# Modulation rows of the next layer formed beside the down projection, sums of weights formed before the up stage, and an eighth bank of products

## The chip, the cores and the metric

One core of a Trainium2 chip runs the whole program. The metric is the device time of one execution in microseconds; the median of several executions is compared. Engines are called PE (TensorE), DVE (VectorE), ACT (ScalarE), POOL (GpSimd) and SP (SyncE, which here only gives out DMAs).

## What is computed

A model of two layers over 1024 latent tokens and 256 context tokens, width 1024. What the change touches is the second half of a layer and the modulation (cut from the reference):

```python
for l in range(DEPTH):                      # DEPTH = 2
    need_ctx = l < DEPTH - 1                # context tokens only in layer 0
    sh1, sc1, g1, sh2, sc2, g2 = jnp.split(cond_lat @ w_mod[l] + b_mod[l], 6, axis=-1)
    csh1, csc1, cg1, csh2, csc2, cg2 = jnp.split(cond_ctx @ w_mod[l] + b_mod[l], 6, axis=-1)
    ...
    h = h + g1 * (mix_lat @ w_out[l])
    h = h + g2 * conv_ffn(modulate(rms_norm(h, norm2_g[l]), sh2, sc2), w_up[l], ..., w_down[l])
def conv_ffn(t, w_up, conv_w, conv_b, w_down):
    u = dwconv(t @ w_up, conv_w, conv_b, FFN_PAD[0], FFN_PAD[1])
    g, v = jnp.split(u, 2, axis=-1)         # D_FF = 2816 columns each
    return (jax.nn.silu(g) * v) @ w_down
```

Inputs and output are float32; w_mod has 1024 x 6144 elements a layer.

## The kernel before, in words

Tokens lie along the free dimension in three chunks: A and B of 512 latent tokens each and c of 256 context tokens (layer 0 alone). A tile is 128 rows of output columns. Every float32 factor is split into a rounded part and a rest (hi and lo, `split`, L318 to 323: ACT writes hi, POOL or DVE subtracts for lo), and a product is three matmuls: hi x hi, hi x lo, lo x hi.

A layer runs in five stages: input projection, attention, out projection (`out_proj`), up (`UpProj`), down (`down_proj`).

**Up.** 22 tiles j, each of a gate half (g, z = 0) and a value half (v, z = 1). The products over the chunks A and B go by seven sub-products (`part`, L196) of 4 x 3 matmuls of 512 columns each, in place of eight: over halves of the contraction, sums and differences of weights (`sums_g`, `sums_v`, names s1 to s4) meet sums and differences of inputs (names t1 to t4, formed by `norm` for chunk B from those of A and B). Parts 1 and 2 need only chunk A's inputs; parts 6, 3, 7, 4, 5 those of chunk B in the order t2, 22, t3, t4, t1. In layer 0 two products over the context (`context`, 24 matmuls of 256 columns) come on top. DVE adds the parts up into `fr`; then the convolution over tokens (`conv`: ACT, two DVE ops on 1282 columns, for g and for v; silu; one multiply) gives y, which is stored to DRAM (`ysp`, L241). Weights come over SP into places of 4096 bytes a partition that are used in turn (`unit`: ten in layer 0, fourteen in layer 1), two for a load with its hi part; `plain` loads and splits, `sums_g` and `sums_v` load, form sums on DVE and POOL and split. `early` loads the first of them in the out stage, `ahead` issues first products while chunk B's norm is still going on. Banks of PSUM are taken in turn from `RING`.

**Down.** Tiles of y and of w_down are fetched two tiles ahead (`fetch`), split, and multiplied in groups of two tiles: for each chunk eight outputs n (slots), 6 matmuls each; DVE adds each bank to h in SBUF (`add`, L316), in the first group ACT copies it to `da` and DVE or POOL adds. The last group, with the norm of the next layer behind it, is the returned function `last`.

**Modulation rows.** `mod_rows(l, js, width, bufs)` is a generator that forms cond @ w_mod of layer 1 without the matmul over k: it loads 128 rows k of w_mod (`mraw`), and DVE multiplies by the column of cond and adds up (`macc`, L567 the first, L316 the others); after eight k a matmul with ones sums over partitions (L580), a copy (L583, `ms`), small transposes (L313) and an add of the bias (L592) bring the row to columns. With js = range(6) and width 512 this is sixteen blocks of eight steps: for j < 2 with 256 columns and two accumulators (latent and context), then with 512 columns and one. A `yield` stands before every step and at the pauses. `run` advances it two steps at four places of a tile; the rest is drawn behind the stage.

Instructions are given to a scheduler that keeps the order of the program roughly and moves them by its own priorities; all engines and SP then run their lists in order. What it did is shown below where it matters.

Of the kernel before, what the change touches and what calls it, by code (L numbers as in the profile page):

```python
# [9 lines left out]
F32 = mybir.dt.float32  # L10
# [44 lines left out]
class UpProj:  # L55
# [6 lines left out]
    RING = (0, 1, 2, 3, 4, 5, 6)  # L62
# [25 lines left out]
    def norm(self, ch):  # L88
# [30 lines left out]
        nc.vector.tensor_tensor(d, b.mod[l][:, 3, 0, 4:8], b.mod[l][:, 3, 0, 0:4], op=OP.subtract)  # L119
        for k in range(4):  # L120
            t1, t2, t3, t4, x2 = (f[q][k] for q in ("t1", "t2", "t3", "t4", "22"))
            scaled(t3, k)
            nc.vector.tensor_tensor(t1, t3, t1, op=OP.subtract)
            scaled(x2, k + 4)
            b.stt(t2, x2, sh(k + 4), t1, OP.add, OP.subtract)
            b.stt(t3, x2, d[:, k:k + 1], t3, OP.add, OP.subtract)
            b.stt(t4, t4, sh(k + 4), t2, OP.add, OP.subtract)
            both("22", k, x2, sh(k + 4))
            for t in ("t2", "t3", "t4", "t1"):
                hi, lo = self.x[t][k]  # L130
                b.split(hi, lo, f[t][k], pool_lo=t in ("t1", "t4"))
# [86 lines left out]
    def ahead(self):  # L218
        for j, n in ((0, 1), (1, 1), (0, 2), (1, 2)):
            self.late.append(self.context(0, n - 1) if self.cs and j else self.part(j, n))  # L220
            yield

    def early(self):
        self.plain(0, 0)
        self.plain(0, 1)
        if not self.cs:
            self.plain(1, 0)

    def conv(self, j, z):
# [11 lines left out]
        b.nc.sync.dma_start(b.ysp[j][:, a0 - PC:a1 - PC], g[:, a0:a1])  # L241

    def run(self, fillers):
# [4 lines left out]

        def fill(n):
            for _ in range(n):  # L250
                next(fillers, None)
        n = 4 if self.cs else 3
        for take in self.late[:n]:
            take()
        for j in range(NH):
            if j == 1:
                for take in self.late[n:]:
                    take()
# [4 lines left out]
            if j:  # L263
                self.plain(j, 1)
            if (self.cs or j) and j < NH - 1:
                self.plain(j + 1, 0)
            if j == 0:
                self.sums_g(0)
                self.sums_v(0)
            if j < NH - 1:  # L270
                self.sums_g(j + 1)
            fill(2)
            self.part(j, 6)()
            self.part(j, 3)()
            if 0 < j < NH - 1:
                self.sums_v(j + 1)
            fill(2)
            self.part(j, 7)()
            self.part(j, 4)()
            if j == 0:  # L280
                self.sums_v(1)
            else:
                self.context(j, 1)()
            fill(2)
            self.part(j, 5)()
            fill(2)
            self.conv(j, 0)
            self.conv(j, 1)


class Builder:
# [249 lines left out]
    def mod_rows(self, l, js, width, bufs):  # L541
# [15 lines left out]
        for i in range(len(bufs)):  # L557
            load(i)
        for i, (j, cs, w, c0, k) in enumerate(todo):
# [10 lines left out]
            load(i + len(bufs))  # L570
            if k < KT - 1:
                continue
            yield
            yield
# [9 lines left out]
            yield  # L584
# [659 lines left out]
    def down_proj(self, l, chunks):  # L1244
# [35 lines left out]
        def group(js, parts, ring, evac):  # L1280
            for ch in parts:
                c0, m = CHUNKS[ch]
                g = self.mod[l][:, 5, 1 if ch == "c" else 0]
                for n in range(KT):
                    ps = self.bank(ring[ch] if isinstance(ring, dict) else ring)[:, :m]
                    self.gemm(ps, [term(j, n, ch) for j in js])
                    evac(n, ch, ps, g[:, n:n + 1], self.h[n][:, c0:c0 + m])
                yield ch
# [61 lines left out]
    def build(self, ctx):  # L1350
# [38 lines left out]
        for l in range(DEPTH):  # L1389
            need = l < DEPTH - 1  # L1390
            chunks = ("A", "B", "c") if need else ("A", "B")
            if l:
                first = self.first_weights(l)
# [56 lines left out]
```

## Time and profile before

| | before |
|---|---|
| runs, us | 3114.69, 3118.12, 3119.87 (median 3118.12) |
| profiled execution, us | 3120.11 |
| its span from the first to the last instruction, us | 3118.3 |
| mean granted clock of TensorE | 0.964 |
| PE, DVE, ACT, POOL busy, us | 2859.0, 2289.3, 1398.5, 1228.1 |
| HBM read and written, MB | 243.02, 54.02 |

A stage is read from the stretches in which its tiles appear: in layer 0 the out projection lies at about 640 to 777 us of the span, the up stage to 1452, the down stage to 1786; in layer 1 the up stage at 2409 to 2846 and the down stage behind it. "Busy" is time in which an engine works on at least one instruction; successive instructions of an engine overlap by some tens of nanoseconds. The granted clock is the share of TensorE's full speed that the profile shows for the stretch: 1.0 is 2.4 GHz, 0.5 is 1.2 GHz.

### The profile page before, as it was taken

What the parts mean: (1) busy time and instruction counts of PE and PEld (TensorE: products, weight loads), DVE (VectorE), ACT (ScalarE), POOL (GpSimd) and SP (SyncE); (2) the same over time, 40 slices, a digit from 0 to 9 for tenths busy, and PEclk for the clock granted to TensorE, in tenths of its full rate; (3) what the DMA queues carried; (4) which work ended last, traced back from release to release, by engine and by line L of the source; (5) the groups of instructions that cost most, each with busy time, mean ns of one, the idle gap of its engine ahead of it and who ended that gap; (6) DMA issues with size and microseconds to landing.
All of it is one profiled execution on the core that took longest, in us unless ns stands there. A gap on an engine that the chain in (4) does not pass through costs nothing.

```text
span 3118.3 us, 38974 instructions
## 1 busy us (share of the span) xinstructions
PE 2859.0 (92%) x14523; PEld 2283.4 (73%) x14523; DVE 2289.3 (73%) x3098; ACT 1398.5 (45%) x2198; POOL 1228.1 (39%) x726
## 2 busy tenths in 40 slices
PE   7999988899789889889999998998899899999998
PEld 4668855578578678767788866876567688887787
DVE  5676798877878787878666767789745876666766
ACT  4675477733323232234211366557753443444213
POOL 1211266542544434444411121137653666665210
PEclk8999999999899899999999999999999899999999
DMA  7413200142234345456312210110022344445221
GB/s 257 137 61 100 64 14 5 44 137 79 87 110 125 104 137 150 129 152 216 135 63 77 75 34 28 50 60 14 21 75 78 88 128 128 122 123 191 95 95 55
DMA packets 295775, 299.57 MB, mean 96 GB/s; under 512 B 16586, under 2 KB 250658, under 8 KB 295586
## 3 DMA queue, kind: packets, MB, share of 16 engines
q1 hardware_dynamic: 295586, 297.09, 29.9%
q8 instruction: 114, 1.87, 0.2%
q14 instruction: 75, 0.61, 0.1%
HBM read 243.02 MB, written 54.02 MB: 95 GB/s over the span
## 4 chain that ended last, share of the span: by engine, by line
PE 52%; DVE 25%; DMA 8%; ACT 7%; issue 5%; POOL 2%; SPq 0%; DVEq 0%; ACTq 0%; POOLq 0%
PE bank L310 51%; DVE cv L316 4%; DMA wr<-in_w_up 3%; DMA mraw<-in_w_mod 3%; ACT lru L307 2%; DVE macc L316 2%; DVE lru L316 2%; DVE mt L994 2%; PE bank L313 1%; ACT cv L307 1%; ACT L307 1%; DVE fr L208 1%; DVE mt L998 1%; DVE xt L323 1%; DVE y L1087 1%
## 5 line engine op out<-in xcount | busy, mean ns | idle before, releaser
L321 POOL TENSOR_TENSOR w<-wr,w 128x1024 fp32r<-128x1024 f32 (+1 forms) x220 | 560.6, 2567 | 518.6 <-ACT w L307 467.4
L310 PE MATMUL bank<-y,w 128*128 128x512 f32 (+1 forms) x2688 | 566.9, 372 | 10.0 <-DVE h L316 9.3
L310 PE MATMUL bank<-xt,w 128*128 128x512 f32 x2112 | 530.7, 405 | 37.2 <-POOL w L321 10.6
L310 PEld LDWEIGHTS bank<-y,w 128*128 128x128 f32 x2688 | 468.7, 190 | 105.2 <-DVE h L316 11.2
L310 PEld LDWEIGHTS bank<-xt,w 128*128 128x128 f32 x2112 | 408.2, 196 | 136.0 <-POOL w L321 14.5
L307 ACT ACTIVATE w<-wr 128x1024 fp32r<-128x1024 f32 (+1 forms) x220 | 223.4, 1018 | 548.3 <-POOL wr L168 377.7
L1054 POOL TENSOR_TENSOR ph<-pf,ph 128x512 fp32r<-128x512 f32 x256 | 341.0, 1354 | 309.2 <-PE bank L310 159.9
L316 DVE SCALAR_TENSOR_TENSOR h<-bank,mod,h 128x512 f32<-128x512 f32 (+1 forms) x448 | 302.9, 687 | 200.3 <-PE bank L310 199.6
L310 PE MATMUL bank<-a,w 128*128 128x512 f32 x1536 | 388.8, 405 | 9.9 <-ACT a L307 2.4
L310 PE MATMUL bank<-x,w 128*128 128x512 f32 x1584 | 394.3, 400 | 2.5 <-DVE fr L208 1.7
L316 DVE SCALAR_TENSOR_TENSOR cv<-fr,fcol,cv 128x1282 f32<-128x1282 f32 (+1 forms) x176 | 320.1, 1877 | 55.0 <-ACT cv L307 55.0
L310 PEld LDWEIGHTS bank<-x,w 128*128 128x128 f32 x1584 | 303.7, 194 | 68.6 <-DVE fr L208 2.6
L310 PEld LDWEIGHTS bank<-a,w 128*128 128x128 f32 x1536 | 287.5, 191 | 85.7 <-issue 11.7
L321 POOL TENSOR_TENSOR w<-raw,w 128x1024 fp32r<-128x1024 f32 x38 | 102.0, 2685 | 422.7 <-ACT w L307 422.7
L310 PE MATMUL bank<-ph,V 128*128 128x512 f32 (+1 forms) x768 | 245.5, 416 | 6.8 <-ACT ph L307 2.9
L316 DVE SCALAR_TENSOR_TENSOR macc<-mraw,cond,macc 128x256 f32<-128x256 f32 (+1 forms) x196 | 182.8, 962 | 37.4 <-DMA mraw<-in_w_mod 36.4
L310 PEld LDWEIGHTS bank<-ac,w 128*128 128x128 f32 x1536 | 196.6, 193 | 16.0 <-issue 5.0
L310 PE MATMUL bank<-ac,w 128*128 128x256 f32 x1536 | 204.3, 287 | 3.3 <-ACT lru L307 1.4
L310 PE MATMUL bank<-w,a 128*128 128x256 f32 x1536 | 200.1, 286 | 3.2 <-ACT gq L307 3.2
L310 PEld LDWEIGHTS bank<-w,a 128*128 128x128 f32 x1536 | 190.2, 191 | 11.0 <-issue 5.7
L994 DVE TENSOR_REDUCE mt<-bank 128x1 f32<-128x512 f32 (+2 forms) x336 | 168.5, 534 | 39.8 <-PE bank L310 37.2
L307 ACT ACTIVATE y<-yr 128x1282 fp32r<-128x1282 f32 (+1 forms) x44 | 51.4, 1169 | 296.8 <-DMA yr<-y_spill 235.1
(206 smaller groups left out, 3923.4 us busy)
## 6 DMA issues: line engine op xcount, KB each, us to landing
wr<-in_w_up SPq DMA_DIRECT2D x154, 512.0 KB
wr<-in_w_down SPq DMA_DIRECT2D x44, 512.0 KB
mraw<-in_w_mod SPq DMA_DIRECT2D x80, 256.0 KB
mraw<-in_w_mod SPq DMA_DIRECT2D x32, 512.0 KB
raw<-in_w_in SPq DMA_DIRECT2D x32, 512.0 KB
y_spill<-cv SPq DMA_DIRECT2D x22, 641.0 KB
yr<-y_spill SPq DMA_DIRECT2D x22, 641.0 KB
y_spill<-cv SPq DMA_DIRECT2D x22, 512.0 KB
```

The costliest lines, as they stand in the source:

```text
L208: add = lambda out, y: nc.vector.tensor_tensor(out, ps, y, op=OP.add)
L307: return self.nc.scalar.activation(out, in_, func, **kw)
L310: return self.nc.tensor.matmul(out, lhsT, rhs, start=start, stop=stop)
L313: return self.nc.tensor.transpose(out, in_, self.ident[:n, :n])
L316: return (eng or self.nc.vector).scalar_tensor_tensor(out, in0, scalar, in1, op0=op0, op1=op1)
L321: self.nc.gpsimd.tensor_tensor(lo, src, hi.bitcast(F32), op=OP.subtract)
L323: self.nc.vector.tensor_sub(lo, src, hi.bitcast(F32))
L994: nc.vector.reduce_max(mt[:, 4 * s + u:4 * s + u + 1], ps[:, :n], axis=AX.X)
L998: nc.vector.tensor_tensor(m, m, mt[:, 4 * s:4 * s + 4], op=OP.max)
L1054: nc.gpsimd.tensor_tensor(pl, pf, ph.bitcast(F32), op=OP.subtract)
L1087: nc.vector.tensor_tensor(y, y, R, op=OP.mult)
```

## The change

1. The modulation rows of layer 1 are no longer drawn in `run` but in the down stage of layer 0, one step (one `next`) after every slot of the first ten groups, with eight buffers instead of two, loads given out two steps later than the buffer is free, and three pauses instead of two and one. `run` loses its fillers.
2. The store of y is given out in the next tile, after part 3, instead of at the end of its own.
3. The ring of banks takes in bank 7, which the modulation rows used.
4. `early` forms the sums for tile 0 as well; in layer 0 the plain value weights of tile 0 are loaded later in return. `ahead` issues the parts of tile 0 and one context product.
5. `norm` of chunk B goes name by name over k instead of k by k, in the order in which parts 6, 3, 7, 4, 5 ask; the difference for t1 is formed on POOL; t4 is formed from the hi and lo of t2 by two ops; the rests of t1 and t4 are taken on DVE.
6. The first weights of layer 1 are asked for before the last group of the down stage instead of behind it.

```diff
-    RING = (0, 1, 2, 3, 4, 5, 6)
+    RING = (0, 1, 2, 3, 7, 6, 5, 4)
...
+        def halves(name, k):
+            b.split(*self.x[name][k], f[name][k])
         for k in range(4):
-            t1, t2, t3, t4, x2 = (f[q][k] for q in ("t1", "t2", "t3", "t4", "22"))
-            scaled(t3, k)
-            nc.vector.tensor_tensor(t1, t3, t1, op=OP.subtract)
-            scaled(x2, k + 4)
-            b.stt(t2, x2, sh(k + 4), t1, OP.add, OP.subtract)
-            b.stt(t3, x2, d[:, k:k + 1], t3, OP.add, OP.subtract)
-            b.stt(t4, t4, sh(k + 4), t2, OP.add, OP.subtract)
-            both("22", k, x2, sh(k + 4))
-            for t in ("t2", "t3", "t4", "t1"):
-                hi, lo = self.x[t][k]
-                b.split(hi, lo, f[t][k], pool_lo=t in ("t1", "t4"))
+            scaled(f["t3"][k], k)
+            nc.gpsimd.tensor_tensor(f["t1"][k], f["t3"][k], f["t1"][k], op=OP.subtract)
+            scaled(f["22"][k], k + 4)
+        for k in range(4):
+            b.stt(f["t2"][k], f["22"][k], sh(k + 4), f["t1"][k], OP.add, OP.subtract)
+            halves("t2", k)
+        for k in range(4):
+            b.stt(f["t3"][k], f["22"][k], d[:, k:k + 1], f["t3"][k], OP.add, OP.subtract)
+            both("22", k, f["22"][k], sh(k + 4))
+        for k in range(4):
+            halves("t3", k)
+        for k in range(4):
+            hi, lo = self.x["t2"][k]
+            b.stt(f["t4"][k], f["t4"][k], sh(k + 4), lo.bitcast(F32), OP.add, OP.subtract)
+            nc.vector.tensor_tensor(f["t4"][k], f["t4"][k], hi.bitcast(F32), op=OP.subtract)
+            halves("t4", k)
+        for k in range(4):
+            halves("t1", k)
...
     def early(self):
         self.plain(0, 0)
-        self.plain(0, 1)
         if not self.cs:
+            self.plain(0, 1)
             self.plain(1, 0)
+        self.sums_g(0)
+        self.sums_v(0)
...
-        b.nc.sync.dma_start(b.ysp[j][:, a0 - PC:a1 - PC], g[:, a0:a1])
+        self.done = lambda: b.nc.sync.dma_start(b.ysp[j][:, a0 - PC:a1 - PC], g[:, a0:a1])
...
-            fill(2)
             self.part(j, 6)()
             self.part(j, 3)()
-            if 0 < j < NH - 1:
+            self.done()
+            if j < NH - 1:
                 self.sums_v(j + 1)
-            fill(2)
             self.part(j, 7)()
             self.part(j, 4)()
-            if j == 0:
-                self.sums_v(1)
-            else:
-                self.context(j, 1)()
-            fill(2)
+            self.context(j, 1)()
             self.part(j, 5)()
-            fill(2)
...
+        lag = 2 if len(bufs) > 4 else 0
+        rest = (3, 3) if lag else (2, 1)
...
-            load(i + len(bufs))
+            if i >= lag:
+                load(i + len(bufs) - lag)
             if k < KT - 1:
                 continue
-            yield
-            yield
+            for _ in range(rest[0]):
+                yield
...
                     evac(n, ch, ps, g[:, n:n + 1], self.h[n][:, c0:c0 + m])
+                    next(fillers, None)
...
-            if l:
-                first = self.first_weights(l)
...
-            fill = self.mod_rows(l + 1, range(6), 512, (self.MS0, self.rope_at + 2048)) if need else iter(())
-            up.run(fill)
-            for _ in fill:
-                pass
-            last = self.down_proj(l, chunks)
+            up.run()
+            fill = self.mod_rows(l + 1, range(6), 512, [self.W0 + 8192 + 2048 * q for q in range(8)])
+            last = self.down_proj(l, chunks, fill if need else iter(()))
+            for _ in fill if need else ():
+                pass
+            if need:
+                first = self.first_weights(l + 1)
```

How the lists of the engines stand is seen at three places (line numbers are 1 to 14 higher in the change; the number at the end of a name counts tiles as they are made).

SP in the middle of the up stage of layer 0, before: `wr<-in_w_up` are loads of weights (of four in a tile, the first is the value half of the sums, and the three others belong to the tile after), `mraw` those of the modulation rows, `y_spill` the store of y.

```order
L141 DMA wr_8540<-in_w_up 128x8x128
L555 DMA mraw_8615<-in_w_mod 128x256
L555 DMA mraw_8619<-in_w_mod 128x256
L555 DMA mraw_8637<-in_w_mod 128x256
L555 DMA mraw_8641<-in_w_mod 128x256
L141 DMA wr_8709<-in_w_up 128x8x128
L141 DMA wr_8703<-in_w_up 128x8x128
L141 DMA wr_8715<-in_w_up 128x8x128
L241 DMA y_spill<-cv_6447 128x1282
L141 DMA wr_8753<-in_w_up 128x8x128
L555 DMA mraw_8777<-in_w_mod 128x256
```

The same place with the change:

```order
L151 DMA wr_7572<-in_w_up 128x8x128
L151 DMA wr_7716<-in_w_up 128x8x128
L151 DMA wr_7710<-in_w_up 128x8x128
L151 DMA wr_7722<-in_w_up 128x8x128
L255 DMA y_spill<-cv_6447 128x1282
L151 DMA wr_7751<-in_w_up 128x8x128
```

The loads of `mraw` are gone from between the loads of weights; the store stands where it stood, behind three loads of weights and ahead of the value half of the sums.

DVE in the down stage of layer 0, in the second group, before: additions of a bank to h, each for a product of its own.

```order
L316 SCALAR_TENSOR_TENSOR h_11538<-bank_60,mod_87,h_11538 128x512
L316 SCALAR_TENSOR_TENSOR h_11539<-bank_61,mod_87,h_11539 128x512
L316 SCALAR_TENSOR_TENSOR h_11540<-bank_62,mod_87,h_11540 128x512
L316 SCALAR_TENSOR_TENSOR h_11541<-bank_63,mod_87,h_11541 128x512
L316 SCALAR_TENSOR_TENSOR h_11542<-bank_64,mod_87,h_11542 128x512
```

With the change, at the end of a block and the start of the next (`ms` is the copy that the transposes on PE wait for, `mod` the finished columns):

```order
L587 COPY ms_11442<-bank_65 128x256
L317 SCALAR_TENSOR_TENSOR h_10884<-bank_63,mod_87,h_10884 128x256
L317 SCALAR_TENSOR_TENSOR h_10885<-bank_64,mod_87,h_10885 128x256
L317 SCALAR_TENSOR_TENSOR h_10886<-bank_58,mod_87,h_10886 128x256
L597 TENSOR_TENSOR mod_88<-bank_65,pcol_84 128x2 x2
L317 SCALAR_TENSOR_TENSOR h_10887<-bank_59,mod_87,h_10887 128x256
L570 TENSOR_SCALAR macc_11476<-mraw_11356,cond_91 128x256
L570 TENSOR_SCALAR macc_11477<-mraw_11356,cond_91 128x256
L317 SCALAR_TENSOR_TENSOR h_10888<-bank_60,mod_87,h_10888 128x256
L317 SCALAR_TENSOR_TENSOR macc_11476<-mraw_11367,cond_91,macc_11476 128x256
L317 SCALAR_TENSOR_TENSOR macc_11477<-mraw_11367,cond_91,macc_11477 128x256
L317 SCALAR_TENSOR_TENSOR h_10889<-bank_61,mod_87,h_10889 128x256
```

Two ops of the modulation rows now stand between two additions, and three additions between the copy and the columns.

DVE in the norm of chunk B in layer 0, before, the list for k = 2 (`xt` and `x` are the tiles of t1 to t4 and 22; the first row is the difference for t1, the last two are rests):

```order
L123 TENSOR_TENSOR xt_1037_6431<-xt_1025_6419,xt_1037_6431 128x512
L316 SCALAR_TENSOR_TENSOR x_1033_6427<-h_5815,gs_89,bank_63 128x512
L316 SCALAR_TENSOR_TENSOR xt_1026_6420<-h_5812,gs_89,bank_63 128x512
L316 SCALAR_TENSOR_TENSOR xt_1029_6423<-x_1033_6427,mod_87,xt_1037_6431 128x512
L316 SCALAR_TENSOR_TENSOR xt_1025_6419<-x_1033_6427,mt_103,xt_1025_6419 128x512
L316 SCALAR_TENSOR_TENSOR xt_1041_6435<-xt_1041_6435,mod_87,xt_1029_6423 128x512
L316 SCALAR_TENSOR_TENSOR x_996_6390<-x_1033_6427,mod_87,x_995_6389 128x512
L323 TENSOR_TENSOR xt_988_6382<-xt_1029_6423,xt_987_6381 128x512
L323 TENSOR_TENSOR xt_980_6374<-xt_1025_6419,xt_979_6373 128x512
```

With the change, from the seventh scaling on:

```order
L317 SCALAR_TENSOR_TENSOR xt_1026_6420<-h_5812,gs_89,bank_63 128x512
L317 SCALAR_TENSOR_TENSOR x_1034_6428<-h_5816,gs_89,bank_63 128x512
L317 SCALAR_TENSOR_TENSOR xt_1027_6421<-x_1031_6425,mod_87,xt_1035_6429 128x512
L317 SCALAR_TENSOR_TENSOR xt_1028_6422<-x_1032_6426,mod_87,xt_1036_6430 128x512
L317 SCALAR_TENSOR_TENSOR xt_1029_6423<-x_1033_6427,mod_87,xt_1037_6431 128x512
L324 TENSOR_TENSOR xt_984_6378<-xt_1027_6421,xt_983_6377 128x512
L324 TENSOR_TENSOR xt_986_6380<-xt_1028_6422,xt_985_6379 128x512
L324 TENSOR_TENSOR xt_988_6382<-xt_1029_6423,xt_987_6381 128x512
L317 SCALAR_TENSOR_TENSOR xt_1030_6424<-x_1034_6428,mod_87,xt_1038_6432 128x512
```

All scalings now come first, and the four tiles that part 6 asks for are finished before those of any other part.

## Rows read from the trace of the kernel before

**Rows 1.** Page, busy us, share of the span and instructions of each engine.

```profile
PE 2859.0 (92%) x14523; PEld 2283.4 (73%) x14523; DVE 2289.3 (73%) x3098; ACT 1398.5 (45%) x2198; POOL 1228.1 (39%) x726
```

**Rows 2.** Stretches; us; busy PE, PEld, DVE, ACT, POOL; clock, DMA share, GB/s.

```profile
777.00:838.00 61.00, 39.83 (x140) 29.19 (x140) 57.93 (x65) 22.72 (x28) 31.17 (x17) 0.77 0.27 80
838.00:1452.50 614.50, 541.62 (x2871) 456.87 (x2869) 482.26 (x489) 187.25 (x204) 270.93 (x121) 0.93 0.45 133
1452.50:1508.00 55.50, 47.74 (x220) 38.00 (x219) 36.13 (x28) 34.30 (x43) 43.59 (x26) 0.93 0.70 242
1508.00:1768.00 260.00, 259.67 (x1320) 220.19 (x1321) 170.68 (x247) 41.60 (x42) 38.24 (x17) 0.99 0.20 73
2409.00:2460.00 51.00, 35.02 (x98) 21.45 (x98) 46.75 (x46) 21.75 (x29) 34.08 (x19) 0.77 0.18 52
2460.00:2846.00 386.00, 386.00 (x1704) 319.57 (x1704) 278.49 (x288) 158.76 (x165) 238.83 (x119) 1.00 0.43 131
```

**Rows 3.** Chain of waits in order of time: start, us, what.

```profile
1508.33 258.98 PE bank L310 x1316
...
2459.73 386.13 PE bank L310 x1703
```

**Rows 4.** Groups on PE, 838 to 1452.5: busy us, mean ns; idle before, releaser.

```profile
L310 PE MATMUL bank<-xt,w 128*128 128x512 f32 x978 | 248.3, 407 | 2.9 <-POOL w L321 2.9
...
L580 PE MATMUL bank<-macc,ones 128*32 128x128 f32 x168 | 7.7, 281 | 2.5 <-DVE macc L316 2.5
L313 PE MATMUL bank<-ident,ms 128*128 128x128 f32 x21 | 6.9, 390 | 67.5 <-DVE ms L583 67.5
```

**Rows 5.** Waits of SP's queue, 838 to 1452.5: us in total, times, longest.

```profile
SPq L555 <- DVE macc L316: 134.1, 91, 5.4
SPq L241 <- DVE cv L240: 111.3, 15, 11.1
```

**Rows 6.** Timeline of PE, two places of the up stage of layer 0.

```profile
846.11 2.88 PE L310 MATMUL bank<-x,w 128*128 128x512 f32 x12
848.83 3.04 PE L310 MATMUL bank<-ac,w 128*128 128x256 f32 x24
851.70 2.91 PE L310 MATMUL bank<-x,w 128*128 128x512 f32 x12
...
1040.31 0.69 PE L313 MATMUL bank<-ident,ms 128*128 128x128 f32 x2 [8.61 <-DVE ms L583]
1040.65 8.20 PE L310 MATMUL bank<-xt,w 128*128 128x512 f32 x24
```

**Rows 7.** Groups on DVE, 838 to 1452.5: busy us, mean ns; idle before.

```profile
L316 DVE SCALAR_TENSOR_TENSOR macc<-mraw,cond,macc 128x512 f32<-128x512 f32 x56 | 69.3, 1238 | 17.8 <-DMA mraw<-in_w_mod 17.5
L316 DVE SCALAR_TENSOR_TENSOR macc<-mraw,cond,macc 128x256 f32<-128x256 f32 x84 | 64.9, 810 | 11.0 <-DMA mraw<-in_w_mod 10.6
```

**Rows 8.** Timeline of DVE, three places of the up stage, one of the down.

```profile
924.88 1.67 DVE L316 SCALAR_TENSOR_TENSOR macc<-mraw,cond,macc 128x256 f32<-128x256 f32 x4
...
1320.42 0.74 DVE L316 SCALAR_TENSOR_TENSOR macc<-mraw,cond,macc 128x512 f32<-128x512 f32 x1
...
1334.65 2.36 DVE L316 SCALAR_TENSOR_TENSOR gs<-mod,pcol 128x4 f32<-128x4 f32 x1
...
1560.11 2.16 DVE L316 SCALAR_TENSOR_TENSOR h<-bank,mod,h 128x512 f32<-128x512 f32 x3
```

**Rows 9.** Timeline of POOL in the down stage of layer 0.

```profile
1559.40 5.41 POOL L321 TENSOR_TENSOR w<-wr,w 128x1024 fp32r<-128x1024 f32 x2 [22.67 <-ACT w L307]
```

**Rows 10.** Timeline of DVE, start and end of chunk B's norm, layer 0.

```profile
767.66 0.75 DVE L316 SCALAR_TENSOR_TENSOR xt<-h,gs,bank 128x512 f32<-128x512 f32 x1 [0.81 <-PE bank L313]
...
799.77 0.68 DVE L168 TENSOR_TENSOR wr<-wr 128x512 f32<-128x512 f32 x1
```

**Rows 11.** Timeline of PE, tile 1 of the up stage of layer 0.

```profile
840.00 3.52 PE L310 MATMUL bank<-ac,w 128*128 128x256 f32 x24
```

**Rows 12.** Timeline of PE, start of the up stage of layer 1.

```profile
2443.26 1.43 PE L310 MATMUL bank<-xt,w 128*128 128x512 f32 x5 [2.08 <-ACT w L307]
```

More of the change, by code (lines that the diff above doesn't have):

```diff
@@ L218, in ahead @@
     def ahead(self):
-        for j, n in ((0, 1), (1, 1), (0, 2), (1, 2)):
-            self.late.append(self.context(0, n - 1) if self.cs and j else self.part(j, n))
+        for j, n in ((0, 1), (0, 2), (1, 1), (1, 2))[:2 if self.cs else 4]:
+            self.late.append(self.part(j, n))
             yield
+        if self.cs:
+            self.late.append(self.context(0, 0))
     def early(self):
         self.plain(0, 0)
-        self.plain(0, 1)
         if not self.cs:
+            self.plain(0, 1)
             self.plain(1, 0)
+        self.sums_g(0)
+        self.sums_v(0)
     def conv(self, j, z):
@@ L240, in conv, with run @@
         b.nc.vector.tensor_mul(g[:, a0:a1], g[:, a0:a1], c[:, a0:a1])
-        b.nc.sync.dma_start(b.ysp[j][:, a0 - PC:a1 - PC], g[:, a0:a1])
-    def run(self, fillers):
+        self.done = lambda: b.nc.sync.dma_start(b.ysp[j][:, a0 - PC:a1 - PC], g[:, a0:a1])
+    def run(self):
         b = self.b
@@ L247, in run @@
                 b.nc.gpsimd.memset(r[:, p:q], 0.0)
[L249 to L253, printed above, removed]
+        for take in self.late[:3]:
             take()
+        self.done = lambda: None
         for j in range(NH):
-            if j == 1:
-                for take in self.late[n:]:
-                    take()
             if j > (0 if self.cs else 1):
@@ L262, in run @@
                 self.part(j, 2)()
-            if j:
+            elif j:
+                self.late[3]()
+            if self.cs or j:
                 self.plain(j, 1)
-            if (self.cs or j) and j < NH - 1:
-                self.plain(j + 1, 0)
-            if j == 0:
-                self.sums_g(0)
-                self.sums_v(0)
+                if j < NH - 1:
+                    self.plain(j + 1, 0)
             if j < NH - 1:
                 self.sums_g(j + 1)
-            fill(2)
             self.part(j, 6)()
             self.part(j, 3)()
-            if 0 < j < NH - 1:
+            self.done()
+            if j < NH - 1:
                 self.sums_v(j + 1)
-            fill(2)
             self.part(j, 7)()
             self.part(j, 4)()
-            if j == 0:
-                self.sums_v(1)
-            else:
-                self.context(j, 1)()
-            fill(2)
+            self.context(j, 1)()
             self.part(j, 5)()
-            fill(2)
             self.conv(j, 0)
             self.conv(j, 1)
+        self.done()
 class Builder:
@@ L583, in mod_rows @@
             nc.vector.tensor_copy(s, ps[:, :P * len(cs)])
-            yield
+            for _ in range(rest[1]):
+                yield
             ps = self.bank((7,))
@@ L1242, in out_proj, with down_proj @@
         return up
-    def down_proj(self, l, chunks):
+    def down_proj(self, l, chunks, fillers):
         nc, io = self.nc, self.io
```

## The prediction

> **What bounds the kernel now.** I read the page first: TensorE (PE) is busy 92% of the span, VectorE (DVE) 73% [rows 1], so the question is where PE's missing time lies. The table of stretches tells it [rows 2]. The down stage of layer 0 (1508 to 1768) has PE busy 259.67 of 260 us at a granted clock of 0.99, the up stage of layer 1 (2460 to 2846) 386 of 386 at 1.00; the chain of waits agrees, with one unbroken piece of PE in each [rows 3]. The up stage of layer 0 has 541.62 of 614.5 us at 0.93, and the two starts of an up stage (777 to 838 and 2409 to 2460) 39.83 of 61 and 35.02 of 51, both at 0.77. So the time to be had lies in the up stage of layer 0 and in the two starts; the down stage has none, and work that goes there must fit beside PE.
>
> What does PE wait for in the up stage of layer 0? Its groups [rows 4] put 67.5 us down to ten of the small transposes of the modulation rows, which wait for the copy of their own sums on DVE, where it is queued behind the convolution; weights are waited for 2.9 us in the largest group. After such a stop the products run slower: 24 of them took 8.20 us after a stop of 8.61 [rows 6], where twelve take 2.72 us (846.11 to 848.83), 0.2267 us each, as in layer 1 (386.13 / 1703 = 0.2267 [rows 3]). The 24 context products take 2.87 us. A tile with 84 products of 512 columns and 48 of 256 then needs 84 x 0.2267 + 2 x 2.87 = 24.8 us. It takes 614.5 / 21 = 29.3.
>
> **The change, part by part.**
>
> *Modulation rows leave the up stage.* All that PE waits for in [rows 4] under the transposes goes, with the slow clock behind it; so do the matmuls of the sums, and DVE loses its macc work, whose two large groups took 69.3 + 64.9 us there [rows 7]. SP loses the loads of mraw, which waited 134.1 us for macc [rows 5] with weight loads queued behind. What is late next is a pair of weights: the sums of the next tile are loaded into places freed by this tile, and pass DVE, POOL, DVE, POOL, ACT and POOL. Layer 1 runs that chain at 19 us a tile without a stop [rows 3], though with more places; layer 0 has 24.8 us for it. I take 0.35 us a tile for it: 25.15 x 21 = 528 us instead of 614.5: **-86**. Ends: -93 (nothing late) and -47 (27 us a tile).
>
> *Sums formed earlier, norm of chunk B in another order.* Before, the first tile's sums start on DVE at 799.77, after the norm that began at 767.66 [rows 10], and the first product of tile 1 ends where its context products follow, at 840.00 [rows 11]; at 2.7 us a product, its start is worth 837.3. Now the sums are done in the out stage. The norm's list on DVE: 8 scalings, 4 + 4 + 4 + 4 scalar ops and 20 plain ones, 0.75 and 0.68 us alone [rows 10] and 0.07 less in a row (four of 0.47 take 1.67 [rows 8]): 24 x 0.68 + 20 x 0.61 = 28.5 us where it took 32.1; the order of the list gives PE its first product after some 13 us and the last after 28.5, at 796. The last two products, the adds and collisions with POOL bring the start of tile 1 to about 805: **-32**, ends -20 and -36. The subtraction that moves to POOL (4 ops) runs under the 8 scalings. In layer 1 PE issued 98 products in 51 us [rows 2], 22.2 us of work; waits for weights such as [rows 12] close it. Its norm ends hardly sooner, but the sums of tile 0 no longer follow it; tile 1's still do: **-8**, ends 0 and -15.
>
> *Modulation rows in the down stage.* Sixteen blocks of eight steps; a step has one scalar op of 512 columns, or two of 256 in the first eight blocks. PE first: in the up stage the matmuls and transposes were busy 7.7 + 6.9 us [rows 4]; all of it now falls into a stage without idle PE. Some of it overlaps what follows; I take +12.
>
> Then DVE. A group of the down stage (two tiles of y, 144 matmuls) takes PE 258.98 / 1316 x 144 = 28.3 us [rows 3]. DVE is busy 170.68 of 260 [rows 2], 18.6 us a group, about 17.3 when ops follow each other (three evacuations take 2.16 us, not 3 x 0.75 [rows 8]). Room: 11. A block with 256 columns costs 16 ops at 0.40 (four took 1.67 us [rows 8]) and small ones, 7.0 us; one with 512 columns 8 x 0.67 (0.74 alone [rows 8]) and small ones, 5.6 us. With pauses a block lasts about 15.5 slots of 24 in a group, so 10.8 us a group in the first half and 8.5 in the second: by these prices it just fits.
>
> But they are the prices with POOL idle. With POOL busy the same ops took 810 and 1238 ns in the mean [rows 7], and an op on 128x4 elements took 2.36 us [rows 8], the length of one POOL split: it was held up whole. In the down stage POOL has one pair of splits a group, 5.41 us [rows 9]. Evacuations read a bank, and three of them ran at full pace (1560.11 [rows 8]) while that pair was running; macc reads two tiles of SBUF. I charge two holds of 2.4 us a group: 17.3 + 10.8 + 4.8 = 32.9 against 28.3 + 1.4 of PE, and 17.3 + 8.5 + 4.8 = 30.6 against 28.3 + 0.8. Over: 3.2 us in 4 groups (in the first ACT evacuates) and 1.5 in 5, 20 us. The first block waits for its loads behind 24 loads of h: +4. **Sum +36**, ends +16 (no holds) and +80 (all 128 + 64 ops at the dear means: 128 x 0.81 + 64 x 1.24 = 183 us, so 17.3 x 9.5 + 183 + 10 = 357 against 269 of PE, less what fits into the first group).
>
> The Trainium skill, SBUF — State Buffer, section "Who interferes with whom", says why: a VectorE instruction with two inputs in SBUF and a GpSimd instruction that reads SBUF shut each other out for the whole instruction, one with a single SBUF input does not. By that rule the holds are paid (+36); without it the stage would cost +16.
>
> What waits behind these: in the down stage the transposes stop PE's products if DVE is over three slots behind, which is the same loss, not another. Loads of mraw wait on SP for macc, with fetches of y and w behind them; those are two groups ahead. The 25 MB of w_mod raise the stage from 73 GB/s by some 90, under the 242 that 1452 to 1508 shows [rows 2].
>
> *At nothing:* the store of y. On SP's list it stood behind the next tile's three weight loads already and stands there still; its wait, 111.3 us in sum [rows 5], shrinks only because DVE has less to do before it. The eighth bank: PE's waits for banks are below what [rows 4] lists; a few us at most either way. First weights of layer 1 ahead of the last group: ACT and POOL are busy 42 and 38 of 260 us there [rows 2], which hides them; without that cover three splits, 8 us.
>
> Sum: -86 - 32 - 8 + 36 = **-90**. The profiled execution took 3120.11 us, 2 above the median of 3118.12; from the median, 3028.
>
> **The rivals.**
> - *DVE takes it all in its stride* (POOL's pair falls where DVE evacuates): down costs 16, time 3008. For it: the evacuations are over half of DVE's work. Against: 2.36 us for a tiny op.
> - *DVE sets the pace of the down stage*, its ops as dear as in the up stage: +80, time 3072. Against: POOL is busy 38 of 260 us there, 271 of 614 in the up stage [rows 2].
> - *The chain of weights sets the up stage*: 27 us a tile, gain 47 instead of 86: 3067. For it: ten places for eight loads a tile. Against: 2.9 us of such waits now.
> - *Slower: the clock.* If PE, stopped by DVE slot after slot, were granted 1.2 GHz instead of 2.4 in the down stage, a group would take 28 us more: 3028 + 28 a group, slower than before from the fourth group on, 3280 with nine. For it: stretches with PE busy 65% had a granted clock of 0.77. Against: at 0.86 busy it was 0.93 [rows 2], and a PE at half speed would no longer outrun DVE, so the stops would cease.
>
> **How the numbers follow.** Forecast 0.56; DVE free 0.15; DVE dear 0.15; weights 0.10; clock 0.04. The range takes in the first three rivals and the ends of the starts: 2990 (free, with -93, -36 and -15) to 3088 (dear, with starts of -20 and -4). A measurement of this kernel tells 0.2% (6 us) from no change. Only the clock is slower: 0.04; a mixture of the dear ends could come to nothing: 0.02; faster 0.94.
>
> **What would show it.** Right: PE in the up stage of layer 0 unbroken, no transposes in it, clock near 1.0, 25 us a tile, down stage beginning some 118 us earlier; in the down stage macc ops of 0.47 and 0.74 us with a few of 2.5 to 3, DVE over 95% busy, PE waiting some 20 us. Wrong: up-stage waits for w of over 1 us a tile; a down stage longer by 60 us or more; a granted clock under 0.9 there.

## The result and the profile after

| | before | after |
|---|---|---|
| median of 4 runs, us | 3118.99 | 3077.32 (3073.86 to 3083.18) |
| ratio, 95% interval | | 0.987 (0.9851 to 0.9889) |
| span of the profiled execution, us | 3118.3 | 3075.1 |

The kernel became 42 us faster: the sign was right and the time lies in the range, but the gain is less than half of the 90 us forecast. Cut at four places on PE, the two profiled executions (and those of three experiments, told below) differ like this; each place is the start of a product, and the down stage of layer 0 is cut at the start of its last product:

| us | before | after | forecast | e1 | e7 | e3 |
|---|---|---|---|---|---|---|
| start of the context product of [rows 11] | 840.0 | 817.0 | -32 | 816.8 | 816.6 | 819.7 |
| from there to the first product of the down stage | 612.9 | 544.1 | -86 | 502.4 | 502.4 | 548.5 |
| products of the down stage, layer 0 | 338.0 | 388.4 | +36 | 379.2 | 358.7 | 335.5 |
| from there to those of layer 1's down stage | 1054.8 | 1051.1 | -8 | 1053.3 | 1049.4 | 1053.2 |
| the rest | 272.7 | 274.6 | 0 | 272.5 | 273.2 | 272.9 |

After: -23.0 - 68.8 + 50.4 - 3.7 + 1.9 = -43.2, the difference of the spans. Every gain came out smaller than forecast and the one loss larger.

Stretches of the kernel after, columns as in [rows 2]; they are its start of the up stage, the up stage and two pieces of the down stage in layer 0, then start and up stage of layer 1:

```profile
777.00:815.00 38.00, 32.75 (x150) 26.19 (x150) 35.00 (x42) 13.58 (x17) 15.47 (x7) 0.96 0.25 70
815.00:1360.80 545.80, 519.09 (x2685) 442.38 (x2684) 368.30 (x287) 185.05 (x205) 287.95 (x120) 0.98 0.38 107
1360.80:1420.00 59.20, 42.34 (x221) 33.67 (x221) 55.03 (x63) 27.91 (x38) 31.52 (x21) 0.88 0.71 240
1420.00:1720.00 300.00, 280.33 (x1497) 229.17 (x1496) 264.66 (x447) 44.01 (x42) 47.82 (x20) 0.96 0.43 141
2372.00:2415.50 43.50, 33.25 (x101) 23.16 (x101) 40.50 (x50) 18.21 (x26) 19.35 (x11) 0.79 0.15 41
2415.50:2800.00 384.50, 384.49 (x1696) 318.48 (x1697) 287.54 (x287) 156.91 (x164) 239.85 (x118) 1.00 0.43 130
```

The up stage of layer 0 rose from 88% busy at 0.93 to 95% at 0.98, but it isn't unbroken: 27 us of PE are idle. The down stage, where PE was idle for 8 us in the first 55 and for none of the 260 behind [rows 2], has 17 us in its first 59 and 20 in the 300 behind. What PE waits for, in the up stage and then from 1360 to 1740:

```profile
PE bank L311 <- POOL w L322: 26.7, 15, 2.8
...
PE bank L584 <- DVE macc L317: 33.9, 10, 13.4
```

The transposes of [rows 4] are gone, as forecast, in both places. In their stead PE waits for weights in the up stage, and in the down stage for the sums of the modulation rows ahead of the matmul with ones.

Who makes the weights late? The waits of SP's queue and of DVE in the same stretch of the up stage (815 to 1360.8):

```profile
SPq L255 <- DVE cv L254: 262.1, 21, 15.2
SPq L151 <- PE bank L311: 222.7, 57, 7.9
```

```profile
DVE wr L178 <- DMA wr<-in_w_up: 81.7, 19, 5.4
DVE cv L317 <- ACT cv L308: 63.5, 20, 3.3
```

The wait of the store for the multiply was 111.3 us [rows 5] and is 262.1 now: the forecast had it shrink. Behind the store stands the value half of the next sums (the order of SP shown ahead of the prediction), and DVE waits 81.7 us for that; before, it was 24.9 (838 to 1452.5):

```profile
DVE wr L168 <- DMA wr<-in_w_up: 24.9, 17, 3.8
```

One tile, on SP, DVE and POOL:

```profile
946.69 0.34 SPq L255 DMA_DIRECT2D y_spill<-cv  x1
947.14 12.63 SPq L151 DMA_DIRECT2D wr<-in_w_up  x4
```

```profile
933.59 11.08 DVE L317 SCALAR_TENSOR_TENSOR cv<-fr,fcol,cv 128x1282 f32<-128x1282 f32 x4 [3.27 <-ACT cv L308]
944.59 0.68 DVE L218 TENSOR_TENSOR fr<-bank,p 128x512 f32<-128x512 f32 x1
945.19 1.48 DVE L254 TENSOR_TENSOR cv<-cv,cv 128x1282 f32<-128x1282 f32 x1
946.59 0.68 DVE L218 TENSOR_TENSOR p<-bank,p 128x512 f32<-128x512 f32 x1
947.37 1.29 DVE L218 TENSOR_TENSOR fr<-bank,p 128x512 f32<-128x512 f32 x2
952.90 0.69 DVE L178 TENSOR_TENSOR wr<-wr 128x512 f32<-128x512 f32 x1 [4.24 <-DMA wr<-in_w_up]
```

```profile
929.85 12.00 POOL L322 TENSOR_TENSOR w<-wr,w 128x1024 fp32r<-128x1024 f32 x4
```

Read in turn: the multiply (L254) ends at 946.67, the store is given out at 946.69, the load behind it at 947.14; DVE stands 4.24 us until it lands, with the sum (L178) at 952.90 and three additions to fr behind it. The sum lets POOL and ACT begin their splits, which are late for PE; and the convolution behind runs beside POOL's four splits and takes 11.08 us, so the next multiply is late too. Read like this the loop is closed: store, load, sum, convolution, multiply, store. From one sum to the next it took 27.2 us (925.68 to 952.90), and PE, which needs 24.8, waits at its end.

That was a reading. The rivals were that the chain of sums and splits itself, with ten places, sets the pace and the store only stands beside it; and for the down stage, that it isn't the rows that cost there, or not by holds of DVE (a hold is an op of DVE that takes longer while POOL works: an add to macc of 256 columns up to 2.7 us instead of 0.48).

### The profile page after: what moved, and what is told of

Read it like the earlier page. It is cut to its first block, busy times and chain, and to the rows that moved or that the text cites. A ratio compares the mean times of both kernels' runs of the same rounds, so it can differ in the third digit from the quotient of the medians.

```text
span 3075.1 us, 38807 instructions
## 1 busy us (share of the span) xinstructions
PE 2847.9 (93%) x14523; PEld 2275.6 (74%) x14523; DVE 2273.6 (74%) x3114; ACT 1391.0 (45%) x2198; POOL 1230.1 (40%) x718
## 5 line engine op out<-in xcount | busy, mean ns | idle before, releaser
L322 POOL TENSOR_TENSOR w<-wr,w 128x1024 fp32r<-128x1024 f32 (+1 forms) x220 | 580.3, 2663 | 471.8 <-ACT w L308 467.5
L311 PE MATMUL bank<-y,w 128*128 128x512 f32 (+1 forms) x2688 | 581.0, 376 | 8.1 <-DVE h L317 5.2
L317 DVE SCALAR_TENSOR_TENSOR cv<-fr,fcol,cv 128x1282 f32<-128x1282 f32 (+1 forms) x176 | 374.8, 2186 | 86.1 <-ACT cv L308 86.1
L311 PE MATMUL bank<-x,w 128*128 128x512 f32 x1584 | 382.3, 392 | 0.7 <-ACT x L308 0.7
L311 PEld LDWEIGHTS bank<-w,a 128*128 128x128 f32 x1536 | 190.3, 191 | 11.1 <-issue 5.7
L311 PE MATMUL bank<-Q,K 128*128 128x512 f32 (+1 forms) x512 | 170.5, 427 | 2.0 <-ACT pf L308 1.7
```

Source lines behind the costliest of these rows:

```text
L311: return self.nc.tensor.matmul(out, lhsT, rhs, start=start, stop=stop)
L317: return (eng or self.nc.vector).scalar_tensor_tensor(out, in0, scalar, in1, op0=op0, op1=op1)
L322: self.nc.gpsimd.tensor_tensor(lo, src, hi.bitcast(F32), op=OP.subtract)
```

## Experiments

All times below are medians of 4 runs, with the ratio to before from runs on the same chip, since before itself was 3117.48 us beside e1 to e4, 3124.45 beside e5 to e8 and 3117.83 beside e9 to e11. So e5 to e8 are compared with others by ratio.

**e1: the store behind the load.**

```diff
-            self.done()
             if j < NH - 1:
                 self.sums_v(j + 1)
+            self.done()
...
         tt(nc.vector, v[:, 4:], v[:, :4], v[:, 4:], OP.add)
+        if self.cs and j > 1:
+            y = self.cv[0][:, PC:PC + 1]
+            b.stt(y, v[:, 4, 0:1], 0.0, y, OP.mult, OP.add)
```

The added op is a tie, which makes the store depend on the load: without it the scheduler keeps the store ahead of the load, whether the program gives it out behind the sums or behind part 5. With it SP's list reads three loads, value half, store:

```
L151 DMA wr_8439<-in_w_up 128x8x128
L151 DMA wr_8433<-in_w_up 128x8x128
L151 DMA wr_8445<-in_w_up 128x8x128
L151 DMA wr_8473<-in_w_up 128x8x128
L258 DMA y_spill<-cv_6447 128x1282
```

> The change, with one tiny op of DVE more in each tile of layer 0's up stage (y's first column plus zero times a value of the new sum), so that the store of y can only be given out behind the load of the value half of the sums and no longer ahead of it; all other lists of engines stand as in the change. Theory S (a loop through the store: the load waits on SP behind a store that waits for the multiply, DVE waits for the load, the next multiply comes late): tiles of layer 0 fall from 27.1 us to 25 to 25.5 us, some 17 tiles by 2 us, about -34, 3043 us; DVE's wait of 4.2 us for the load at the sum goes. Rival C (the chain of sums and splits itself, through POOL and through ten places, sets 27 us; the store is only in the queue beside it): within 5 us of 3077. Rival K (the store, later, ends after the next convolution wants its buffer): ACT waits for the store, slower than 3077 by up to 1 us a tile, 3098.

Measured: 3026.37 us, ratio 0.9705 (0.9682 to 0.9728), 51 us below the change. The up stage of layer 0 from the context product of [rows 11] on, then DVE's wait for the load over 815 to 1319, then two sums that follow each other:

```profile
817.00:1319.00 502.00, 502.00 (x2675) 435.16 (x2675) 338.05 (x308) 190.13 (x207) 264.94 (x122) 1.00 0.39 121
```

```profile
DVE wr L178 <- DMA wr<-in_w_up: 12.3, 18, 1.2
```

```profile
914.82 0.69 DVE L178 TENSOR_TENSOR wr<-wr 128x512 f32<-128x512 f32 x1 [0.47 <-DMA wr<-in_w_up]
...
939.89 0.69 DVE L178 TENSOR_TENSOR wr<-wr 128x512 f32<-128x512 f32 x1 [0.69 <-DMA wr<-in_w_up]
```

PE has no gap at all, at full clock, with ten places as before. Sums follow at 25.1 us (914.82 to 939.89); 41.6 us less in this stage, and 9.2 less in the down stage, whose first group begins with less left over (41.3 us instead of 47.6). Theory S holds, larger than expected; C and K fall. Since the lists of PE, ACT and POOL are those of the change, DVE's too but for the tiny op (0.20 us in the mean, once a tile), and only the store has moved on SP, this is the store's doing.

**e2: rows from the eight last slots of the first group on.**

```diff
-                    next(fillers, None)
+                    if js[0] or ch == "c":
+                        next(fillers, None)
```

> The change, with the modulation rows drawn from the last eight slots of the down stage's first group on (chunk c) instead of from its first slot. Theory F (the first block is squeezed: its last two macc stand on DVE behind eight additions of da, and PE waits 13.4 us for them): the wait goes, -13, 3064 us, first group 34 to 36 us instead of 47.6. Rival D (DVE has too much to do in the stage as a whole, the wait is only where it shows first): the groups after it lengthen by as much, 3077 within 4 us. Rival E (the last block now ends at the last slot and its transposes stop PE there): 3064 plus 3 to 5.

Measured: 3079.38 us, ratio 0.9881 (0.9863 to 0.9899): no gain. The wait at the first matmul with ones, and the one that took its place at the next group's transposes (the change, then e2):

```profile
1398.09 1.08 PE L584 MATMUL bank<-macc,ones 128*32 128x128 f32 x16 [13.37 <-DVE macc L317]
```

```profile
1406.32 5.49 PE L311 MATMUL bank<-y,w 128*128 128x512 f32 x12 [4.42 <-ACT da L308]
1424.65 0.69 PE L314 MATMUL bank<-ident,ms 128*128 128x128 f32 x2 [7.65 <-DVE ms L587]
```

The first group takes 30.2 us instead of 47.6, the second 47.6 instead of 39.1, the eight behind 262.9 instead of 258.8: the stage is 3 us shorter, which the time doesn't show. Rival D holds. So the 13.4 us read as a debt of DVE that is paid at whichever block comes first.

**e3: no modulation rows of layer 1.**

```diff
-            fill = self.mod_rows(l + 1, range(6), 512, [self.W0 + 8192 + 2048 * q for q in range(8)])
+            fill = iter(())
+            if need:
+                self.nc.vector.memset(self.mod[1], 0.5)
+                self.nc.vector.memset(self.gs[1], 0.5)
```

> The change without the modulation rows of layer 1: they are left out, and constants of 0.5 stand in their place. Theory T (all that the down stage lost is the price of the rows): the stage goes back from 379 to about 328 us, the time to 3077 - 50 = 3027 us, and groups after the first take 28.1 us. Rival U (a part is the fetches, the early first weights of layer 1 or the clock after the up stage): the stage stays above 340 us, the time above 3039. By the prediction's term of 36 it would be 3041.

Measured: 3029.86 us, ratio 0.9722 (0.9704 to 0.9741). The program leaves the rows of layer 1 out. Its down stage is 335.5 us, 2.5 below before's, the eight groups behind the second 28.0 to 28.1 us each. Theory T: all that the stage lost is the price of the rows, and the early first weights of layer 1 cost nothing.

**e4 and e8: the two halves of the start undone.** e4 has the old body of `norm` for chunk B (the removed lines of the change's diff in place of the added ones); e8:

```diff
             self.plain(1, 0)
-        self.sums_g(0)
-        self.sums_v(0)
...
+            if j == 0:
+                self.sums_g(0)
+                self.sums_v(0)
```

with the sums of tile 1 behind its second context product, as before.

> The change with the list of chunk B's norm as it was before, all else as changed. Theory N (half of what the starts gained is the norm's order: DVE's 3.6 us less and first products 13 us after its beginning): tile 1 of layer 0 starts 10 us later, layer 1's start 5 us later, 3092 us. Rival M (the sums formed in the out stage carry the whole start): 3077 within 4 us. Rival O (the new list, with its rests on DVE and its plain ops held by POOL, is the dearer one): 3067.

> The change with tile 0's sums formed in the up stage again instead of in the out stage (the units in the order of before, the sums of tile 1 behind the second context product). Theory Q (the start's gain of 23 us in layer 0 is the norm's order, 10 by e4, and the early sums, the rest): tile 1 starts 13 us later, 3089 to 3093 us. Rival M (the sums are hidden behind the norm's list anyway): 3077 within 4.

Measured: e4 3087.87 us, ratio 0.9909 (0.9892 to 0.9925); e8 3083.23 us, ratio 0.9874 (0.9857 to 0.9892). In the traces the product of [rows 11] starts at 825.3 in e4 and 828.0 in e8 (817.0 in the change, 840.0 before). Part of these differences lies ahead of anything that was edited: a run of 44 products early in the out stage starts at 645.1 in the change, 649.1 in e4, 647.9 in e8 and 649.5 before, and at 643.0 to 650.1 in the other programs. Before, then the change:

```profile
649.50 10.16 PE L310 MATMUL bank<-a,w 128*128 128x512 f32 x44
```

```profile
645.14 10.16 PE L311 MATMUL bank<-a,w 128*128 128x512 f32 x44
```

From there to the product of [rows 11] it is 190.5 us before, 171.9 in the change, 176.2 in e4 and 180.1 in e8; e1, e2, e3, e7 and e9 to e11, which have the change's start, need 170.7 to 172.3. So the edits of the start are worth 18.6 us in layer 0, of which undoing the norm's order takes back 4 and undoing the early sums 8; what makes the other 6 isn't shown. In layer 1, from the first product of the out stage to the first of the down stage, it is 540.7 us before, 537.4 in the change, 539.3 in e4 and 537.4 in e8: 3.3 in all, 1.9 of it the norm's order. The time shows the norm (the intervals of e4 and the change lie apart), by some 12 us, more than these two terms; of the early sums it shows nothing, because e8's down stage happened to be 8 us shorter.

**e5 and e6: the rows back in the up stage, the store behind the load.** Both on e1: `run` has its fillers again and bank 7 leaves the ring.

```diff
-            up.run()
-            fill = self.mod_rows(l + 1, range(6), 512, [self.W0 + 8192 + 2048 * q for q in range(8)])
+            fill = self.mod_rows(l + 1, range(6), 512, (self.MS0, self.rope_at + 2048)) if need else iter(())
+            up.run(fill)
```

e6 moreover has `rest = (3, 4)` and draws 3, 3, 3 and 2 steps.

> The kernel of e1 with the modulation rows back where they were before the change: drawn two at four places of a tile in layer 0's up stage, two buffers, pauses of two and one, bank 7 taken out of the ring for them. Theory B (the small transposes wait for a copy behind the convolution whatever the store does, 67.5 us in all before): the down stage goes back to some 330 us (-50), the up stage from 24.8 to 28 us a tile or more (+70 to +90), 3045 to 3065 us, so the move itself was worth 20 to 40. Rival A (it was the store that kept DVE and so the transposes late, and the move was worth nothing): 25.5 us a tile, 3026 - 50 + 15 = 2991 us.

> As e5, with pauses of three steps ahead of the matmul with ones and four ahead of the transposes, drawn three, three, three and two at a tile's four places. Theory P (what costs in the up stage is only that the transposes come a convolution too soon): PE waits less than 10 us for the copy, the up stage 522 to 530 us, and the time falls under e1's: 2990 to 3005 us. Rival W (loads of w_mod that wait on SP for macc hold up the weight loads, and macc waits for POOL's splits): 27 us a tile, 3025 to 3045.

Measured: e5 3081.33 us, ratio 0.9862 (0.9845 to 0.9878); e6 3066.58 us, ratio 0.9814 (0.9799 to 0.9828). PE's waits from 820 to 1420, e5 and e6:

```profile
PE bank L324 <- DVE ms L597: 52.2, 8, 11.6
PE bank L594 <- DVE macc L327: 5.1, 3, 2.5
```

```profile
PE bank L594 <- DVE macc L327: 30.5, 12, 5.0
PE bank L324 <- DVE ms L597: 18.4, 5, 6.6
```

Theory B holds for e5: the transposes stop PE whatever the store does, and the move alone is worth 0.0157 of the time, 49 us (e5 against e1), dearer to undo than was expected. The longer pauses of e6 take 34 us off that wait and put 25 on the one ahead of it; P falls. W names the wait that came, macc, but its time is exceeded too. Against e6 the move is worth 0.0109, 34 us. So the move of the rows was right with the store behind the load; with the store at its old place it wasn't run by itself, and the two stages between which the rows moved gained 18 us together in the change (-68.8 + 50.4).

e5 also tells what the store's place cost before: with the rows in the up stage and the store behind the load that stage takes 593.1 us (827.9 to 1421.0) where before's took 612.9. So up to 20 us of the loop's price were there already; in the change it is 42.

**e7: the rests of w_down formed on DVE in layer 0.** On e1:

```diff
-            self.split(wh, wl, wr, pool_lo=True)
+            self.split(wh, wl, wr, pool_lo=not cs)
```

> The kernel of e1 with the rest of the down stage's weights formed on DVE instead of POOL in layer 0. In e1 POOL's 22 splits held 17 macc, which took 1.79 us in the mean, some 20 us in all more than unheld ones; as ops of DVE the rests cost some 1.2 us each, 22 to 26 us. Theory L (holds cost what the trace shows): 3026 within 5 us. Rival H (holds of 2.4 us twice a group, as predicted): 2.4 us a group back, 3004. Rival V (DVE's order suffers, y and w come later): 3040.

Measured: 3006.69 us, ratio 0.9621 (0.9606 to 0.9635), against e1's 0.9705: 20 us less by the medians, 26 by the ratios, and 20.5 in the trace of the down stage (358.7 us instead of 379.2). PE's wait for macc in the whole stage (1318 to 1690, 1318 to 1670) and the ten groups with rows, columns as in [rows 2]: e1, then e7.

```profile
PE bank L587 <- DVE macc L320: 31.8, 10, 10.3
...
1319.24:1655.50 336.26, 303.50 (x1657) 247.72 (x1655) 305.29 (x492) 63.88 (x67) 73.56 (x38) 0.96 0.50 162
```

```profile
PE bank L587 <- DVE macc L320: 11.1, 4, 6.6
...
1319.05:1634.90 315.85, 302.08 (x1658) 246.97 (x1656) 296.14 (x512) 64.20 (x67) 22.03 (x17) 0.98 0.52 170
```

The largest groups of macc on DVE and what the matmul with ones waits for, in 300 us (1378 to 1678): e1, then e7, where this stretch reaches the stage's end.

```profile
L320 DVE SCALAR_TENSOR_TENSOR macc<-mraw,cond,macc 128x512 f32<-128x512 f32 x56 | 48.0, 856 | 0.0
L320 DVE SCALAR_TENSOR_TENSOR macc<-mraw,cond,macc 128x256 f32<-128x256 f32 x84 | 47.5, 605 | 0.0
...
L587 PE MATMUL bank<-macc,ones 128*32 128x128 f32 x160 | 8.7, 305 | 19.6 <-DVE macc L320 19.5
```

```profile
L320 DVE SCALAR_TENSOR_TENSOR macc<-mraw,cond,macc 128x512 f32<-128x512 f32 x56 | 41.8, 747 | 0.0
...
L320 DVE SCALAR_TENSOR_TENSOR macc<-mraw,cond,macc 128x256 f32<-128x256 f32 x76 | 33.3, 480 | 0.0
...
L327 DVE TENSOR_TENSOR w<-wr,w 128x1024 fp32r<-128x1024 f32 x16 | 19.3, 1219 | 0.0
...
L587 PE MATMUL bank<-macc,ones 128*32 128x128 f32 x160 | 8.1, 285 | 2.2 <-DVE macc L320 2.2
```

PE waits 20.7 us less for macc, all of what the stage gained. DVE has 20 rests of 1.22 us more to do in the ten groups and yet is busy for 296.1 us instead of 305.3: without POOL's splits its other ops are shorter by more than the rests cost. Theory L, which put the holds at some 20 us, falls; H's time came. What DVE saves is 9 of the 20 us that the stage gained. That the others come because a hold is one piece of over 2 us in the middle of a block, which the block's last step passes on to PE, while a rest is an op of 1.2 us that finds room, is a reading that no run tests.

**e9, e10, e11: on e7.** e9 takes bank 7 out of the up stages' ring (`RING = (0, 1, 2, 3, 6, 5, 4)`), e10 has e2's edit, e11 `rest = (5, 2)`.

> The kernel of e7 with the ring of seven banks that the kernel before had (the eighth taken out of the up stages). Theory Z (the bank is worth nothing, as predicted: PE runs unbroken at 24.8 us a tile and DVE is never seven products behind): ratio to before within 0.0015 of e7's 0.9621. Rival Y (while DVE is in the convolution, 6 to 11 us at 2.7 us a product, PE runs out of banks): 1 us a tile, +20 us, ratio 0.968 or more.

> The kernel of e7 with the rows drawn from chunk c of the first group on, as in e2. In e7 PE still waits 11.1 us for macc, 6.6 of it at the first block. Theory F2 (now that no split of w holds DVE, the first block's wait goes and none takes its place): -6, ratio 0.960. Rival D2 (as in e2: the wait comes back one group later, or the last block ends too late): within 0.0015 of 0.9621.

> The kernel of e7 with five pauses instead of three ahead of the matmul with ones and two instead of three ahead of the transposes, all slots used. Theory G (PE waits for macc because the matmul stands too close behind the last step in PE's list): of the 11.1 us all but the first block's 6.6 goes, -4 us, ratio 0.961; the tail of the last block before the last group gives 2 back. Rival D3 (what is late is the macc chain as a whole, more slots between don't help): within 0.0015 of 0.9621 or above.

Measured: e9 3004.94 us, ratio 0.9638 (0.9619 to 0.9657); e10 3017.06, 0.9676 (0.9660 to 0.9692); e11 3007.12, 0.9644 (0.9623 to 0.9666). The eighth bank is worth nothing: in e9 PE is busy 500.00 of 500.00 us from 817 to 1317 (the ratio is 0.0017 off e7's, just over the 0.0015 allowed, with intervals that overlap). Rows drawn later cost 10 us by the medians and 17 by the ratios; F2 falls, and PE waits 9.2 us for the first copy. The longer pause takes PE's waits for macc from 11.1 to 5.5 us and makes others of 3.0 for the copy and 4.3 for a bank; no change. e7 is the best version, with e9 and e11 level.

## Why the prediction was right, and where it failed

*The step that failed: "At nothing: the store of y".* It said that the store's place on SP's list is the old one and that its wait shrinks. The place is indeed the old one. But the wait grew from 111.3 to 262.1 us, since with the modulation rows gone the loop through that store became the slowest loop of the stage; before, PE's stops for the transposes hid half of it (e5) and DVE waited 24.9 us for the load, 81.7 now. The price hung on the term "0.35 us a tile" for the chain of weights: measured, (544.1 - 5.6) / 20 = 26.9 us a tile, 2.1 above the least, and e1 shows that the store's place makes all of it, 42 us in the up stage and 9 in the down stage. The rival "the chain of weights sets the up stage, 27 us a tile" had the pace right, with a chance of 0.10, and the cause wrong: it blamed ten places, and e1 runs without a stop in ten.

*A count in the same term was wrong too.* The stretch was divided by 21 tiles, as the row at 840.00 [rows 11] was read as standing behind the first product of tile 1. It is the second context product of that tile, with one part of it to come. The stretch holds twenty tiles, a context product and one part: 20 x 24.8 + 2.87 + 2.72 = 501.6, and e1's PE is busy for 502.00 with 2675 products (20 x 132 + 36 = 2676). With 25.15 us a tile the gain should have read -104, not -86; against that, -68.8 came. Half of the miss was hidden by the miscount.

*That e1 meets the forecast is luck.* With the store behind the load the kernel is 0.0295 of the time, 92 us, faster than before, where 90 were forecast. But its parts are -110 in the up stage, +41 in the down stage and -25 in the starts, not -86, +36 and -40.

*The down stage: cause right, size off by 14, the accounting in part luck.* The rows are the cause (e3), and holds are a part of it. The prediction had +16 without holds and +36 with them. Measured against e3's 335.5: +53 in the change, +44 in e1, +23 in e7, where POOL's splits no longer hold DVE. That holds make 20 in the forecast and e7 gains 20.5 on e1 is partly luck: e7 takes the holds away and gives DVE 24 us of rests, and the forecast's sum was of work for which DVE has no time, with DVE over 95% busy; it was busy 264.66 of 300 us, 88%, while PE waited 19.1 us for macc. The Trainium skill, SBUF — State Buffer, section "Who interferes with whom", which the prediction weighed, agrees with the traces on which ops are held: macc of 256 columns, with two inputs in SBUF, took 605 ns in the mean in e1, where POOL splits, and 480 in e7, where it doesn't; additions from a bank 745 and 748. Against e3 the rows cost the first group 11.1 us (47.6 and 36.5), where the forecast had the loads' 4 and 1.4 of PE's own, and the nine behind it 42, where 31 were forecast. Of the 42, some 20 are PE's waits for macc and 14 the rows' own matmuls and transposes (9.0 and 5.0 in 300 us); the other 8 aren't accounted for, but the granted clock there is 0.96 and in e3 0.99. In the first group DVE does the additions of da, and its list puts eight of them ahead of the block's last two macc:

```profile
1378.52 10.05 DVE L317 SCALAR_TENSOR_TENSOR macc<-mraw,cond,macc 128x256 f32<-128x256 f32 x12
1388.49 9.15 DVE L1321 TENSOR_TENSOR h<-h,da 128x512 f32<-128x512 f32 x8
1397.57 0.87 DVE L317 SCALAR_TENSOR_TENSOR macc<-mraw,cond,macc 128x256 f32<-128x256 f32 x2
```

The late up stage adds to it: its last multiply on DVE begins 16 us after PE's last product there (1377.1 and 1360.8), in e1 11 us (1329.6 and 1319.0), and e1's first group is 6.3 us shorter.

*The starts: direction right, size off.* The table has -23 for -32 and -3.7 for -8; counted from the out stages, -18.6 and -3.3. The order of the norm gave 4 + 2 and the early sums 8. The list of DVE was costed as if PE's first products followed it without gaps, but from 777 to 815 PE is busy 32.75 of 38.00 us; that is 5 of the 13 us missing, and the others stay open.

*Right:* the transposes gone, the move worth making (49 us by e5, with the store behind the load), the eighth bank and the early first weights at nothing. The rival of the slow clock did not come: the granted clock is 0.96 in the 300 us of the down stage, between the levels of 1.2 and 2.4 GHz but near the upper. Two signs of being wrong that the prediction named did come: waits for w in the up stage of over 1 us a tile (26.7 us in twenty tiles), and a granted clock under 0.9 in the down stage, though only in its first 59 us (0.88 with 17 us idle, where before had 0.93 [rows 2]).

## What to carry to other kernels

When the largest wait of a stage is removed, what limits it next need not be the next in the list of waits; here it was a loop. Look for a DMA that waits for a result and has loads of a later tile queued behind it, and follow it round, because its wait can grow when the rest gets faster (111.3 to 262.1 us here). An edit in the program that doesn't move a row in the queue's list changes nothing there; a dependency can be needed to move it. Where DVE fills up, price an operation with two inputs in SBUF by what POOL does beside it: moving work from POOL to a DVE that is 88% busy was a gain of 20 us here (e7).

## What was not expected of the hardware

The rests of w cost less on DVE, which was the busier engine, than on POOL: moved over, they took 24 us of DVE's time, DVE's busy time in the ten groups fell by 9 us and PE's wait by 20.7 (e1 and e7). The convolution seems to feel POOL as well, though no run tests it alone: its op of 1282 columns took 2797 ns in the mean in the change and 2301 in e1, where, in the tile looked at, POOL's four splits came in three pieces (4.76, 2.41 and 3.35 us) instead of in one row of 12.00 us:

```profile
L317 DVE SCALAR_TENSOR_TENSOR cv<-fr,fcol,cv 128x1282 f32<-128x1282 f32 x80 | 219.1, 2797 | 63.5 <-ACT cv L308 63.5
```

```profile
L320 DVE SCALAR_TENSOR_TENSOR cv<-fr,fcol,cv 128x1282 f32<-128x1282 f32 x80 | 179.4, 2301 | 50.0 <-ACT cv L311 50.0
```
